# Three blocks of each down projection in Strassen's way, half of the weight sums made by adding transfers

## The chip, the core and the metric

The kernel runs on one core of one Trainium2 chip. The metric is device time in microseconds of one execution, as the median of several runs. The core has five engines that matter here: TensorE (PE; its weight loads are PEld), VectorE (DVE), ScalarE (ACT), GpSimd (POOL) and SyncE (SP), which issues most of the transfers. Sixteen DMA engines carry out the transfers of all queues. SBUF is the working memory; PSUM holds eight banks of 128 x 512 float32 into which PE accumulates.

## The reference

The program is a two-layer decoder trunk on 256 tokens of width 1024, in float32. Each layer has a half-step SwiGLU FFN, a mixing stage (two kinds of attention side by side), a second half-step FFN, and a gated embedding:

```
h = h + 0.5 * (silu(norm(h) @ Wg) * (norm(h) @ Wu)) @ Wd     # FFN 1, width 2816
h = h + concat(stick_breaking(u), latent_attention(u)) @ Wo   # u = norm(h)
h = h + 0.5 * FFN2(norm(h))
h = h + sigmoid(norm(h) @ Wpg) * (p[i] @ Wp)
```

The change concerns the product with Wd (2816 x 1024), the down projection, which occurs four times: FFN "a" and FFN "b" of two layers.

## The kernel before

Every float32 product is made of three: each operand x is split into a high part xh (x rounded to the type that PE reads) and a rest xl = x - xh, and `mm3` (L176 to L178) issues xh*yh, xh*yl and xl*yh into one PSUM bank. The weights arrive as float32 and are split on the core. A *unit* is 2048 columns of 128 rows, in two pieces of 1024 (512 KB). `Unit.load` issues the transfer of a piece on SP's queue into a tile of the pool `raw` (four buffers, L126), copies it to `wh` on ScalarE (L130) and subtracts into `wl` on VectorE (L131); `wh` and `wl` have six buffers each. One piece is one *chunk* of the down projection: 128 rows of Wd by all 1024 columns.

`ffn` first makes the gates, in six blocks of 512 of the 2816 columns (the last has 256). Per block it runs `g` and `u` matmuls for two token halves (t = 0, 1; 128 tokens each). `gated` multiplies silu(g) by u, and `Gates.add` turns the result over: four transposes on PE into a bank `ft` (L373), a copy into `fh` (L376), a subtract into `fl` (L377). So block i of the gates lies in SBUF as 4 chunks of 128 rows by 256 tokens.

Then comes the down projection with four PSUM banks `d[t][n]` (token half t, column half n). Per chunk, `down_mm` issues 2 x 3 matmuls for each token half, 12 in all. After the first two chunks `flush` runs what is still due of the gates; `lagging` runs the other 20 chunks, the second token half three chunks behind the first, so that the residual step of the first half (L313, `h` plus half of `d`, then norm and transposes) overlaps matmuls of the second.

The order of instructions is not simply that of the program. A planner at build time places instructions on each engine by program order among those that it holds ready, grants buffers, and adds the waits. `soon`, `tick` and `flush` delay some steps by an estimated PE time; `after` adds a pure order edge. Once built, each engine runs its list in order; SP's transfers wait in SP's list for their buffer.

`ple_inputs` (L757 to L763) loads and splits the embedding input p of the layer; it stands in the program between the mixing stage and FFN b. The mixing stage keeps its latent tiles under tags of their own: `cq`, `xq`, `ckv`, `xkv`, `qr`.

Of the kernel before, what the change touches and what calls it, by code (L numbers as in the profile page):

```python
# [9 lines left out]
F32 = mybir.dt.float32  # L10
F32R = mybir.dt.float32r
# [6 lines left out]
P = 128  # L18
# [12 lines left out]

F_TAGS = ("sbq", "sbk", "v", "vm", "n0h", "n0l", "n1h", "n1l", "f4h", "f4l", "f5h", "f5l")
# [11 lines left out]
def trunk(ctx: ExitStack, tc: tile.TileContext, xT, xr, pT, w, gains, fgain, consts, out):  # L44
# [3 lines left out]
    raw_p = pool("raw", 4)  # L48
# [58 lines left out]
    class Unit:  # L107
# [36 lines left out]
        def at(self, k, c0, c1):  # L144
            q, o = k // self.per, k % self.per * self.cols
            i = o * self.sub // PIECE
            if (q, i) not in self.here:
                self.here.add((q, i))
                self.load(q, i)
            return tuple(t[:, o + c0 : o + c1] for t in self.parts[q])  # L150

# [4 lines left out]
    def soon(us, f):  # L156
        due.append((pe[0] + us, len(due), f))
# [23 lines left out]
    def both(x, *ix):  # L181
        return tuple(t[ix] for t in x)
# [161 lines left out]
    class Gates:  # L344


        def __init__(self, tag):
            self.tag, self.f = tag, {}
# [14 lines left out]

        def add(self, i, t, pr, more):

            f = self.block(i)
            n = 4 if i < NBLK - 1 else 2

            def go():
                a = bank(f"ft_{self.tag}_{i}{t}")[:, : n * P]  # L370
                behind = newest_mm[0]
                for j in range(n):
                    after(nc.tensor.transpose(a[:, j * P : (j + 1) * P], pr[:, j * P : (j + 1) * P], ident), behind)  # L373
                a = a.rearrange("p (a b) -> p a b", a=n)
                fh, fl = both(f, slice(None), slice(None), slice(t * P, (t + 1) * P))
                nc.scalar.activation(fh, a, AF.Copy)  # L376
                nc.vector.tensor_tensor(fl, a, fh.bitcast(F32), ALU.subtract)  # L377

            soon(1.3 + 0.9 * t + more, go)

    def ffn(x, n, tag, gcol, between=None, feed=None):
# [13 lines left out]
        for i in range(NBLK):  # L395
# [42 lines left out]
            for r in rests:  # L438
                r()
        if between is not None:  # L440
            between()
        d = four(f"d_{tag}")
        us = [Unit(2) for _ in range(DFF // 256)]
        chunks = [(us[k // 2], k % 2, k) for k in range(DFF // P)]
        for c in range(2):
            u, j, k = chunks[c]
            for t in range(2):
                down_mm(d, u, j, gates(k), gates.at(k), t, c == 0, False)
        flush()
        return lagging(chunks[2:], d, gates, 0.5, tag, gcol, 3, False)  # L450

    def mix(x, n, L, g0):
# [93 lines left out]
        cq = at_p.tile([P, 2, T], F32, tag="cq", name=f"cq{L}")  # L546
        nc.vector.tensor_tensor(cq, la, bc(rstd, 2), ALU.mult)
        xq = tuple(at_p.tile([P, 2, T], F32R, tag=f"xq{q}", name=f"xq{q}{L}") for q in "hl")
# [10 lines left out]
        ckv = at_p.tile([P, 1, T], F32, tag="ckv", name=f"ckv{L}")  # L559
        nc.vector.tensor_tensor(ckv[:, 0], la[:, 0], rstd, ALU.mult)  # L560
        xkv = tuple(at_p.tile([P, 1, T], F32R, tag=f"xkv{q}", name=f"xkv{q}{L}") for q in "hl")
# [81 lines left out]
        qr = at_p.tile([P, 2, T], F32, tag="qr", name=f"qr{L}")  # L643
# [113 lines left out]
    def ple_inputs(L):  # L757
        pr = at_p.tile([P, 2, T], F32, tag="cq", name=f"p{L}")
        nc.sync.dma_start(pr, pT[L])
        xp = tuple(at_p.tile([P, 2, T], F32R, tag=f"xq{q}", name=f"xp{q}{L}") for q in "hl")  # L760
        nc.scalar.activation(xp[0], pr, AF.Copy)
        nc.vector.tensor_tensor(xp[1], pr, xp[0].bitcast(F32), ALU.subtract)
        return xp  # L763
# [74 lines left out]
    for L in range(DEPTH):  # L838
# [3 lines left out]
        xp = ple_inputs(L)  # L842
        x, n = ffn(x, n, f"b{L}", g0 + G_PLE)
# [10 lines left out]
def _weights(i):  # L854
# [9 lines left out]
    for L in range(DEPTH):  # L864
# [5 lines left out]
        def ffn(n):  # L870
# [7 lines left out]
            units.extend(cols(wd[k : k + 256], ar(DM)) for k in range(0, DFF, 256))  # L878
# [81 lines left out]
```

## Time and profile before

| | |
|---|---|
| median of 3 runs | 1039.98 us (1039.97 to 1040.15) |
| the profiled execution | 1040.93 us |
| its span in the profile | 1039.1 us |
| TensorE busy | 1022.7 us, 98% |
| VectorE busy | 616.4 us, 59% |
| ScalarE busy | 571.2 us, 55% |
| GpSimd busy | 8.2 us, 1% |
| read from memory | 185.45 MB, 179 GB/s over the span |

"Busy" is the time in which an engine had at least one instruction in work. Matmuls are pipelined: a row gives each 0.39 us, while the next one starts before it ends. In rows of a timeline the first number is the start in the span, the second the length, and the bracket says how long the engine had been idle and what ended that. In rows of groups, "x176 | 69.2, 393 | 0.0" is the count, the busy sum, the mean in ns and the idle time before.

### The profile page before, as it was taken

Reading aid. Unit: us, or ns where it says so; the run is one execution under the profiler, and the core shown is the slowest. Engines: PE = TensorE matmul, PEld = TensorE weight load, DVE = VectorE, ACT = ScalarE, POOL = GpSimd, SP = SyncE. Lnnn points to the kernel's source line nnn. Section 1 sums busy time; section 2 is a strip of 40 time slices with the busy share of each in tenths; the row PEclk is TensorE's granted clock in tenths of the full one; section 3 lists DMA queues with packets and bytes.
Section 4 is the critical chain, followed back from the end, with each engine's and each line's share of the span. In section 5 each row is a group of like instructions: output and inputs, shape, how many; then the busy total and the mean of one; then the engine's idle time right before and its main releaser. Section 6 shows DMA issues by size and latency. Waiting matters only on the chain.

```text
span 1039.1 us, 13656 instructions
## 1 busy us (share of the span) xinstructions
PE 1022.7 (98%) x5178; PEld 863.3 (83%) x5178; DVE 616.4 (59%) x855; ACT 571.2 (55%) x869; POOL 8.2 (1%) x13
## 2 busy tenths in 40 slices
PE   9999999999999999999999999999999999999996
PEld 7688888899888888888888888888997888888885
DVE  5565544766776555546875555448677755554475
ACT  5854444758565544435764455347766744444464
POOL 0000000000100000000000000000000000000000
PEclk9999999999999999999999999999999999999998
DMA  7775545565146555555465555456633465554551
GB/s 235 282 245 185 184 158 195 192 216 178 64 147 205 190 183 184 181 164 201 165 219 186 182 183 182 164 199 215 209 107 111 144 219 184 184 182 162 189 197 40
DMA packets 53490, 187.39 MB, mean 180 GB/s; under 512 B 6064, under 2 KB 6192, under 8 KB 53424
## 3 DMA queue, kind: packets, MB, share of 16 engines
q1 hardware_dynamic: 52992, 185.95, 53.7%
q8 instruction: 40, 0.66, 0.3%
q10 hardware_dynamic: 432, 0.57, 0.2%
q14 instruction: 26, 0.21, 0.1%
HBM read 185.45 MB, written 1.05 MB: 179 GB/s over the span
## 4 chain that ended last, share of the span: by engine, by line
PE 91%; ACT 3%; DMA 2%; DVE 2%; issue 1%; SPq 0%; ACTq 0%
PE g_b L178 4%; PE g_b L176 4%; PE g_b L177 4%; PE d_b L177 4%; PE d_b L178 4%; PE d_b L176 4%; PE d_a L176 4%; PE d_a L177 4%; PE d_a L178 4%; PE g_a L178 4%; PE g_a L176 4%; PE g_a L177 4%; PE u_b L176 3%; PE u_b L177 3%; PE u_b L178 3%; PE u_a L177 3%
## 5 line engine op out<-in xcount | busy, mean ns | idle before, releaser
L131 DVE TENSOR_TENSOR wl<-raw,wh 128x1024 fp32r<-128x1024 f32 (+1 forms) x354 | 424.1, 1202 | 351.6 <-ACT wh L130 350.7
L130 ACT ACTIVATE wh<-raw 128x1024 fp32r<-128x1024 f32 (+1 forms) x354 | 366.6, 1041 | 366.3 <-PE d_a L178 64.4
L176 PE MATMUL d_a<-wh,fh_a 128*128 128x512 f32 x176 | 69.2, 393 | 0.0
L176 PE MATMUL d_b<-wh,fh_b 128*128 128x512 f32 x176 | 69.2, 393 | 0.0
L178 PE MATMUL d_a<-wh,fl_a 128*128 128x512 f32 x176 | 68.6, 390 | 0.0
L178 PE MATMUL d_b<-wh,fl_b 128*128 128x512 f32 x176 | 68.6, 390 | 0.0
L177 PE MATMUL d_a<-wl,fh_a 128*128 128x512 f32 x176 | 68.5, 389 | 0.0
L177 PE MATMUL d_b<-wl,fh_b 128*128 128x512 f32 x176 | 68.5, 389 | 0.0
L178 PEld LDWEIGHTS d_a<-wh,fl_a 128*128 128x128 f32 x176 | 33.0, 188 | 7.0
L178 PEld LDWEIGHTS d_b<-wh,fl_b 128*128 128x128 f32 x176 | 33.0, 188 | 6.9
L177 PEld LDWEIGHTS d_a<-wl,fh_a 128*128 128x128 f32 x176 | 33.1, 188 | 6.7
L176 PEld LDWEIGHTS d_b<-wh,fh_b 128*128 128x128 f32 x176 | 33.0, 188 | 6.6
L177 PEld LDWEIGHTS d_b<-wl,fh_b 128*128 128x128 f32 x176 | 33.1, 188 | 6.6
L176 PE MATMUL g_b<-wh,x_mix1h 128*128 128x512 f32 x96 | 38.4, 400 | 0.0
L176 PE MATMUL g_b<-wh,x_mix0h 128*128 128x512 f32 x96 | 38.4, 400 | 0.0
L176 PEld LDWEIGHTS d_a<-wh,fh_a 128*128 128x128 f32 x176 | 33.1, 188 | 6.5
L176 PE MATMUL g_a<-wh,xe0h 128*128 128x512 f32 x96 | 38.4, 400 | 0.0
L176 PE MATMUL g_a<-wh,x0h 128*128 128x512 f32 x96 | 38.1, 398 | 0.3 <-ACT x0h L221 0.3
L177 PE MATMUL g_a<-wl,x0h 128*128 128x512 f32 x96 | 37.5, 393 | 0.3 <-DVE wl L131 0.2
L178 PE MATMUL g_a<-wh,xe0l 128*128 128x512 f32 x96 | 37.5, 391 | 0.0
L178 PE MATMUL g_b<-wh,x_mix0l 128*128 128x512 f32 x96 | 37.5, 390 | 0.0
L178 PE MATMUL g_b<-wh,x_mix1l 128*128 128x512 f32 x96 | 37.5, 390 | 0.0
(383 smaller groups left out, 2282.8 us busy)
## 6 DMA issues: line engine op xcount, KB each, us to landing
raw<-in_w SPq DMA_DIRECT2D x338, 512.0 KB, 3.6
raw<-in_w SPq DMA_DIRECT2D x16, 256.0 KB, 4.0
xin<-in_xT SPq DMA_DIRECT2D x4, 256.0 KB, 3.5
h<-in_xr SPq DMA_DIRECT2D x2, 512.0 KB, 7.6
p<-in_pT SPq DMA_DIRECT2D x2, 256.0 KB, 4.5
fg<-in_fgain SPq DMA_DIRECT2D x1, 512.0 KB, 3.2
out_h<-hg SPq DMA_DIRECT2D x2, 256.0 KB, 2.3
out_h<-hg ACTq DMA_DIRECT2D x2, 256.0 KB, 2.7
```

Source lines behind the costliest of these rows:

```text
L130: nc.scalar.activation(wh[:, a], r[:, a], AF.Copy),
L131: nc.vector.tensor_tensor(wl[:, a], r[:, a], wh[:, a].bitcast(F32), ALU.subtract),
L176: nc.tensor.matmul(o, ah, bh, start=start, stop=False, **kw)
L177: nc.tensor.matmul(o, ah, bl, start=False, stop=False, **kw)
L178: newest_mm[0] = nc.tensor.matmul(o, al, bh, start=False, stop=stop, **kw)
```

## The change

In blocks 1, 2 and 3 of each FFN, four chunks (512 rows of Wd) are treated as one product of 256 x 512 activations by 512 x 1024 weights, cut in half in each direction. Winograd's form of Strassen's scheme makes it of 7 products of a quarter (each 128 tokens x 256 rows x 512 columns, six matmuls) instead of 8. Products 2, 3 and 4 go straight into three of the `d` banks; products 1, 5, 6 and 7 get a bank each, summed over the three blocks, and are combined once after the third.

- *Activations.* `Gates.sums` forms four sums of quarters after the transposes of token half 1 (one copy and four VectorE instructions of 128 x 512, then two copies and two subtracts as splits). Those of blocks 1 and 2 lie in a pair of the x buffers, those of block 3 in new tiles `s0h`, `s0l`. For token half 1, only the second two chunks of these blocks are still split.
- *Weights.* `Seven` loads the four quarters b11, b12, b21, b22 (512 KB each, stored as such), and makes 7 operands: b11, b22, b21 as loaded, b12 + b22, b11 + b12, that plus b22, and that plus b21; the signs are taken into the activations. The first two sums are made by transfers issued on POOL that add a quarter from memory to the tile (`accum_op`), the last two by VectorE. Each operand is copied and subtracted as before.
- *Order.* Two plain chunks, block 1, two plain chunks, block 2, the two chunks of the short last block, block 3, the combination into `h`, then the four chunks of block 4 in `lagging`. The weights in memory follow this order.
- *Room.* `raw` has six buffers instead of four; the latent tiles and p move under the tags `s0h`, `s0l`, `s1h`, `s1l`; the scratch for transfers issued by POOL is set to 2048; `ple_inputs` now runs behind the combination of FFN b.

```diff
-    raw_p = pool("raw", 4)
+    raw_p = pool("raw", 6)
...
+    class Seven:
...
+        def load(self, i):
+            self.raw[i] = raw_p.tile([P, PIECE], F32, tag="raw", name=f"raw7_{self.u}_{i}")
+            newest_load[0] = nc.sync.dma_start(self.raw[i], self.home(i))
...
+        def fetch(self, i, j):
+            nc.gpsimd.dma_start(self.raw[i], self.home(j), accum_op=ALU.add)
+        def add(self, i, j):
+            nc.vector.tensor_tensor(self.raw[i], self.raw[i], self.raw[j], ALU.add)
+        def parts(self, i):
...
+            newest_wh[0] = nc.scalar.activation(wh, r, AF.Copy)
+            nc.vector.tensor_tensor(wl, r, wh.bitcast(F32), ALU.subtract)
+            return wh, wl
+        def operands(self):
+            b11, b12, b21, b22 = range(4)
+            self.load(b12)
+            self.fetch(b12, b22)
+            self.load(b11)
+            yield 1, self.parts(b11)
+            self.fetch(b11, b12)
+            self.load(b22)
+            yield 3, self.parts(b22)
+            self.load(b21)
+            yield 2, self.parts(b21)
+            yield 7, self.parts(b12)
+            yield 5, self.parts(b11)
+            self.add(b11, b22)
+            yield 6, self.parts(b11)
+            self.add(b11, b21)
+            yield 4, self.parts(b11)
...
+    def seven_mm(banks, x_of, ops, first, last):
+        for p, (wh, wl) in ops:
+            for j in range(2):
+                c = slice(j * 512, (j + 1) * 512)
+                mm3(banks[p], x_of(p, j), (wh[:, c], wl[:, c]), first(p) and j == 0, last(p) and j == 1, skip_group_check=True)
...
+        head, tail = block(0), block(NBLK - 1)
+        plain(head[:2], True)
+        flush()
+        p = {2: d[0][0], 3: d[0][1], 4: d[1][0]}
+        p.update((i, bank(f"p{i}_{tag}")) for i in (1, 5, 6, 7))
+        own = (1, 5, 6, 7)
+        for i in SEVEN:
+            seven_mm(p, gates.seven(i), Seven().operands(), lambda q: q in own and i == SEVEN[0], lambda q: q in own and i == SEVEN[-1])
+            if i != SEVEN[-1]:
+                plain(head[2:] if i == SEVEN[0] else tail)
...
+        u, v, a, b = (flat(f"w{k}", f"{m}7_{tag}") for k, m in enumerate("uvab"))
+        nc.scalar.copy(u, p[1])
+        nc.vector.tensor_tensor(u, u, p[6], ALU.add)
+        to_h(0, 0, p[1])
+        nc.vector.tensor_tensor(v, u, p[7], ALU.add)
+        to_h(1, 0, v)
+        nc.vector.tensor_tensor(a, p[5], u, ALU.subtract)
+        to_h(0, 1, a)
+        nc.vector.tensor_tensor(b, p[5], v, ALU.subtract)
+        to_h(1, 1, b)
         if between is not None:
             between()
...
+        rest = [c for i in range(1, NBLK - 1) if i not in SEVEN for c in block(i)]
+        return lagging(rest, d, gates, 0.5, tag, gcol, 3, False)
...
-    nc = bacc.Bacc("TRN2", target_bir_lowering=False, num_devices=1)
+    nc = bacc.Bacc("TRN2", target_bir_lowering=False, num_devices=1, dynamic_dma_scratch_size=2048)
```

More of the change, by code (lines that the diff above doesn't have):

```diff
@@ L362, in at, with sums, seven, of @@
             return k % 4
+        def sums(self, i):
+            a, b = self.turned[i, 0], self.turned[i, 1]
+            lo, hi = slice(0, 2), slice(2, 4)
+            e = SEVEN.index(i)
+            if e == 0:
+                self.spare = tuple(x_p.tile([P, KC, T], F32R, tag=f"x{q}", name=f"sx{q}_{self.tag}") for q in "hl")
+            if e < 2:
+                out = both(self.spare, slice(None), slice(4 * e, 4 * e + 4))
+            else:
+                out = tuple(f_p.tile([P, 4, T], F32R, tag=f"s0{q}", name=f"s{q}_{self.tag}_{i}") for q in "hl")
+            two = [wt(f"w{2 + k}", f"sum{k}_{self.tag}_{i}") for k in range(2)]
+            s1, s2, s3, s4 = (two[k // 2][:, k % 2].rearrange("p (a b) -> p a b", a=2) for k in range(4))
+            nc.scalar.copy(s3, b[:, lo])
+            nc.vector.tensor_tensor(s1, s3, b[:, hi], ALU.subtract)
+            nc.vector.tensor_tensor(s2, s1, a[:, lo], ALU.subtract)
+            nc.vector.tensor_tensor(s3, a[:, lo], s3, ALU.subtract)
+            nc.vector.tensor_tensor(s4, s2, a[:, hi], ALU.add)
+            for k in range(2):
+                sh, sl = both(out, slice(None), slice(2 * k, 2 * k + 2))
+                nc.scalar.activation(sh, two[k], AF.Copy)
+                nc.vector.tensor_tensor(sl, two[k], sh.bitcast(F32), ALU.subtract)
+            self.s[i] = out
+        def seven(self, i):
+            f, s = self.f[i], self.s[i]
+            t0, t1 = slice(0, P), slice(P, T)
+            def of(p, j):
+                if p in (1, 2, 4):
+                    return both(f, slice(None), j + 2 * (p != 1), t1 if p == 4 else t0)
+                return both(s, slice(None), {5: 0, 6: 1, 7: 2, 3: 3}[p], slice(j * P, (j + 1) * P))
+            return of
         def add(self, i, t, pr, more):
@@ L642, in mix @@
         nc.vector.tensor_tensor(r2, qs[3], bc(rc[:, 1], 2), ALU.mult)
-        qr = at_p.tile([P, 2, T], F32, tag="qr", name=f"qr{L}")
+        qr = at_p.tile([P, 4, T], F32, tag="s1l", name=f"qr{L}")[:, 0:2]
         nc.gpsimd.tensor_tensor(qr, r1, r2, ALU.add)
@@ L877, in ffn, with down @@
             wide(np.concatenate([wg[:, m], wu[:, m]], axis=1), ar(512))
-            units.extend(cols(wd[k : k + 256], ar(DM)) for k in range(0, DFF, 256))
+            def down(b):
+                units.extend(cols(wd[k : k + 256], ar(DM)) for k in range(512 * b, min(512 * b + 512, DFF), 256))
+            down(0)
+            down(NBLK - 1)
+            for b in SEVEN:
+                for k in (512 * b, 512 * b + 256):
+                    units.append(np.concatenate([cols(wd[k : k + 256], ar(c, c + 512)) for c in (0, 512)], axis=1))
+            for b in range(1, NBLK - 1):
+                if b not in SEVEN:
+                    down(b)
         ffn("ffn1")
```

57 lines of the change are left out of this document (36 added, 21 removed).

## The prediction

> **What bounds the kernel now.** I read the page's busy times and its chain of waits first, then stretches of the down projections, then single instructions there.
>
> ```profile
> span 1039.1 us, 13656 instructions
> ...
> PE 1022.7 (98%) x5178; PEld 863.3 (83%) x5178; DVE 616.4 (59%) x855; ACT 571.2 (55%) x869; POOL 8.2 (1%) x13
> ...
> PE 91%; ACT 3%; DMA 2%; DVE 2%; issue 1%; SPq 0%; ACTq 0%
> ```
>
> TensorE is the bound: 98% busy, 91% of the chain. A matmul taken out shortens the kernel, as long as nothing else becomes late. The next view gives stretches (length, then busy time of PE, PEld, DVE, ACT, POOL, the granted clock, the DMA share, GB/s): the middle of the first down projection, a gate stretch with more work around it, and the fullest stretch of transfers.
>
> ```profile
> 140.00:185.00 45.00, 45.00 (x201) 37.24 (x200) 18.81 (x17) 15.91 (x15) 0.00 (x0) 1.00 0.56 184
> 45.00:66.00 21.00, 21.00 (x102) 17.41 (x101) 17.84 (x21) 15.56 (x19) 0.00 (x0) 1.00 0.80 263
> 25.00:40.00 15.00, 14.67 (x64) 11.27 (x62) 7.24 (x14) 9.28 (x17) 0.00 (x0) 1.00 0.96 367
> ```
>
> In the down projection PE never stops, at full clock, while VectorE works 42% and the DMA engines 56% of the time. The second row shows that VectorE at 85% (17.84 of 21.00) still cost PE nothing.
>
> A matmul's row says 0.39 us, but matmuls overlap; what one costs is the distance of their starts:
>
> ```profile
> 185.62 1.06 ACT L130 ACTIVATE wh<-raw 128x1024 fp32r<-128x1024 f32 x1 [1.66 <-PE d_a L178]
> 185.64 0.39 PE L177 MATMUL d_a<-wl,fh_a 128*128 128x512 f32 x1
> ...
> 187.00 0.39 PE L177 MATMUL d_a<-wl,fh_a 128*128 128x512 f32 x1
> ...
> 188.34 1.06 ACT L130 ACTIVATE wh<-raw 128x1024 fp32r<-128x1024 f32 x1 [1.66 <-PE d_a L178]
> ```
>
> The two PE rows are six matmuls apart (each third one has L177, and one of that line lies between): 1.36 us, so 0.227 us each. ScalarE takes a new chunk every 2.72 us, the 12 matmuls of a chunk, and waits each time for PE to give a pair of weight buffers back:
>
> ```profile
> ACT wh L130 <- PE d_a L178: 64.4, 34, 5.7
> ```
>
> So weights are converted six pairs ahead of PE. This lead is what the change spends.
>
> **The matmuls.** A block of four plain chunks is 48 matmuls, 10.88 us. In Strassen's way it is 7 products of 6: 42, or 9.52 us. Three blocks in each of four FFNs: 12 x 1.36 = **16.3 us less**. Against the profiled execution (1040.93 us, 1.83 beyond its span) that is 1024.6; against the median of the runs, 1039.98, it is 1023.7. I carry the differences to the median.
>
> **VectorE and ScalarE in such a block.** The prices:
>
> ```profile
> L131 DVE TENSOR_TENSOR wl<-raw,wh 128x1024 fp32r<-128x1024 f32 x338 | 413.4, 1227 | 339.8 <-ACT wh L130 339.1
> L130 ACT ACTIVATE wh<-raw 128x1024 fp32r<-128x1024 f32 x338 | 356.5, 1060 | 356.9 <-PE d_a L178 64.4 <-PE d_b L178 64.4 <-PE u_b L178 44.9
> ...
> L390 DVE SCALAR_TENSOR_TENSOR pr_b<-u_b,hr_mix,s_b 128x512 f32<-128x512 f32 x20 | 14.0, 743 | 0.0
> ...
> L377 DVE TENSOR_TENSOR fl_a<-ft_a,fh_a 128x512 fp32r<-128x512 f32 x20 | 13.7, 687 | 1.7 <-ACT fh_a L376 0.8
> ...
> L376 ACT ACTIVATE fh_a<-ft_a 128x512 fp32r<-128x512 f32 x20 | 11.8, 590 | 5.9 <-PE ft_a L373 5.9
> ```
>
> Seven operands instead of four are copied and subtracted, and two sums are added by VectorE (a 128x1024 add, priced as the subtract): 9 x 1.23 = 11.1 us of VectorE and 7 x 1.06 = 7.4 of ScalarE, beside 9.52 of PE. VectorE is over PE inside the block; with the two plain chunks that follow (2.46 against 5.44) it is 13.5 against 14.96. Throughput holds over a period; order and latency decide.
>
> **The transfers.** Landing times of 512 KB loads, in the stretches 25 to 40, 45 to 66 and 140 to 185 us:
>
> ```profile
> raw<-in_w SPq DMA_DIRECT2D x6, 512.0 KB, 6.7
> ...
> DMA to landing us min/median/max: 4.2/6.7/8.0
> ...
> raw<-in_w SPq DMA_DIRECT2D x11, 512.0 KB, 4.6
> ...
> raw<-in_w SPq DMA_DIRECT2D x15, 512.0 KB, 4.3
> ```
>
> At share 0.96 the engines moved 367 GB/s, so a full rate of 382: 1.37 us for 512 KB. Landing is 4.3 us at share 0.56, 4.6 at 0.80, 6.7 at 0.96. A period after the change has six loads and two adding transfers. The trace has no adding transfer and none issued by POOL. If adding costs as a load, the share is 8 x 1.37 / 14.96 = 0.73; if it also reads what it adds to, 10 x 1.37 / 14.96 = 0.92. I take the row at 0.80, 4.6 us, for a load, and X = 4.6 + 1.37 (the second reading) + 0.33 (an issue, as SP's below) = **6.3 us** for an adding transfer from its release to its landing. Its bounds: below, the fastest load of this stretch, 4.2; above, 6.7 + 1.37 + 0.33 = 8.4.
>
> [...]
>
> **The chain that becomes late.** In one block the tile of b11 goes: load, copy and subtract (product 1), adding transfer, copy and subtract (5), add, copy and subtract (6), add, copy and subtract (4). Its next use needs a buffer: of six raw tiles the block holds four and the plain chunks two, so the next block's b11 waits for the one that the first add gives back. Written out with the prices above, zero being PE's start on the first plain chunk:
>
> ```
>                           block 1   block 2   block 3
> b11 landed (+4.6)          early     10.84     27.70
> product 1 subtracted       early     13.28     30.14
> sum landed (+6.3)          early     19.58     36.44
> pair 5 ready / wanted       5.0/10.9  21.9/25.8  38.7/40.8
> first add done              6.24     23.10     39.96
> pair 6 ready / wanted       8.5/12.2  25.4/27.2  42.3/42.2
> pair 4 ready / wanted      12.1/13.6  28.9/28.6  45.8/43.5
> ```
>
> ("Wanted" is PE undelayed: the blocks start at 5.44, 20.40 and 35.36, products 1.36 us apart. In block 1 the copy of pair 5 starts when the first chunk's pair is free, 2.72.) The lead is eaten in blocks 1 and 2; block 3's last product comes 2.3 us late. What is queued behind a late sum: on ScalarE the copies, on VectorE the subtracts of the same pairs, then those of the next plain chunks. PE has other work meanwhile, the last block's chunks for the first token half, which write other banks than product 4 (d[1][0]) but need subtracts of the same VectorE: I take half as covered, 1.1 us lost per FFN.
>
> **After the third block** one copy and seven VectorE instructions (about 0.69 each by L377) put the products into h: 4.8 us, beside four plain chunks (10.88 of PE, 4.9 of VectorE). They fit, but stand ahead of those chunks in the program: from 0 to 4.8 us; I take 0.4, since the sum of 9.7 is under 10.88.
>
> So 1.5 us of each 4.08 are lost: 4 x 2.6 = 10.3 us gained.
>
> **Costed at nothing.** The sums of activations add six VectorE instructions of 0.69 and three ScalarE ones of 0.59 per block, less half of one split: VectorE goes from 8 x 1.23 + 2 x 0.74 + 2 x 0.69 = 12.7 to 16.5 us in the 21.8 of a gate block's 96 matmuls, 76%, under the 85% that cost nothing above; uncovered, 3.8 us per block. All eight banks are in use from block 1: the last transposes must be read out before product 5 or 6; uncovered, under 2 us per FFN. Half of the x buffers, and the tags shared with the latent tiles, are last read by products long done. The inputs p move behind the products (per layer 0.33 us of SP, 0.63 of ScalarE, 0.68 of VectorE, needed only a stage later); their rows, and one of the output projection wo:
>
> ```profile
> L759 SPq DMA_DIRECT2D p<-in_pT x2: 327/327/327, 247.5 to 758.2; - x2
> L761 ACT ACTIVATE xph<-p x2: 627/627/627, 267.4 to 778.1; 128x512 fp32r<-128x512 f32 x2
> L762 DVE TENSOR_TENSOR xpl<-p,xph x2: 674/675/676, 271.8 to 782.6; 128x512 fp32r<-128x512 f32 x2
> ...
> L176 PE MATMUL wo<-wh,y0h x32: 389/389/499, 276.4 to 303.6; 128*128 128x512 f32 x32
> ```
>
> In the program they stand behind all of wo, whose first matmul is at 276.4, yet the load ran at 247.5 and the split at 267.4 and 271.8: the planner takes what is ready. So I expect SP's loads for the last block ahead of the new p load, which must wait until block 3's sums of activations are read.
>
> **Rivals.**
> 1. *Everything hides*: X is 4.6 or less. Gain 16.3: 1023.7. For: VectorE's 13.5 of 14.96. Against: landing at share 0.80 is 4.6 already without adding.
> 2. *The gain is eaten*: each us of X comes twice by block 3 (blocks 2 and 3), so the loss is 1.5 + 2 (X - 6.3); it reaches 4.08 at X = 7.6: 1040. The p load held in program order ends there too: the last block's loads behind it would start with product 6's end, 43.5, and land and convert by 43.5 + 0.3 + 4.6 + 2.3 = 50.7 against 44.9 wanted, 5.8 us in two FFNs, 11.7 together: 1041.
> 3. *Slower, the sums land too late*: past X = 7.6 the wait for the adding transfer, on ScalarE's copy of pair 5, takes the place of PE. At X = 8.4 the loss is 5.7 per FFN, 1.6 more than the gain: 1046.5. For: 6.7 us at share 0.96 and a share of up to 0.92 here; the planner's order is fixed ahead, so ready subtracts stand behind the late one. Against: the lead of six pairs.
>    [...]
> 4. *Much slower, the adding itself*: an adding transfer that keeps the engines five times as long needs 16 x 1.37 = 21.9 us in each period of 14.96: three times 6.9 less 4.08, four times: +67, 1107. Nothing in the trace speaks for it or against it.
>
> **Numbers.** My forecast of 10.3 us, **1029.7**, has 0.44, with 1025.5 to 1037.5 as its own range (X from 5.3 to 7.2, or the h sums half exposed). Rival 1 has 0.20, rival 2 0.08, rival 3 0.20, rival 4 0.08. A measurement of this kernel can tell about 0.2%, 2.1 us, from no change. Faster: 0.44 + 0.20 = 0.64; same 0.08; slower 0.28. The range runs from full hiding, 1023.5, to rival 3's 1046.5; outside lie rival 4 and part of rival 3, under 0.2.
>
> **What would show it.** The matmuls fall by 12 x 6 = 72 from 5178. Right: PE without idle in block 1, idle of about 1.5 us at the end of block 3, ended by a subtract; adding transfers landing in 5.3 to 7.2 us. Rival 1: none of that idle. Rivals 3 and 4: ScalarE's copies ended by DMA in every block 2 and 3, and a DMA share over 0.9. Wrong altogether: idle in the gate stretches (the activation sums), or SP's loads behind p in the second and fourth FFN.

## The result: slower by 5.3%, and the profile after

The changed kernel takes **1095.09 us** (median of 4 runs, 1094.97 to 1097.6) against 1040.07 us for the kernel before in the same session: a ratio of 1.0527, with a 95% interval of 1.0514 to 1.0539. Forecast were 1029.7 us, and 1023.5 to 1046.5 as the range. The profiled execution took 1095.11 us, 54.2 more than the profiled one of before. Its page, cut to the lines that answer to those shown of before:

```profile
span 1093.3 us, 13847 instructions
...
PE 1040.9 (95%) x5106; PEld 861.7 (79%) x5106; DVE 731.8 (67%) x1019; ACT 617.9 (57%) x945; POOL 28.3 (3%) x37
...
q1 hardware_dynamic: 52992, 185.95, 50.7%
q0 software_dynamic: 3456, 12.58, 6.7%
...
PE 73%; DVE 10%; ACT 7%; DMA 6%; issue 3%; SPq 0%; ACTq 0%; DVEq 0%
...
raw<-in_w SPq DMA_DIRECT2D x338, 512.0 KB, 4.1
raw<-in_w POOLq DMA_DIRECT2D x24, 512.0 KB, 7.0
```

The matmuls fell by 72, as they should. But PE's share of the chain fell from 91% to 73%, and VectorE, ScalarE and DMA share 23%: PE is no longer the bound all the way. Where this happens the four down projections show, each from its first matmul to the first of the next stage. First the kernel before (its sum over the four), then the kernel after; columns as in the prediction: length, busy PE, PEld, DVE, ACT, POOL, granted clock, DMA share, GB/s.

```profile
sum 245.40, PE 245.40 PEld 203.03 DVE 117.86 ACT 111.35 POOL 0.00; mean PE 61.35 PEld 50.76 DVE 29.46 ACT 27.84 POOL 0.00
```

```profile
133.00:205.50 72.50, 64.38 (x260) 48.69 (x260) 51.25 (x56) 36.17 (x47) 3.46 (x4) 0.93 0.65 184
440.80:516.30 75.50, 66.75 (x260) 51.43 (x259) 52.45 (x60) 36.98 (x47) 3.45 (x4) 0.89 0.66 188
670.80:742.40 71.60, 63.45 (x260) 48.35 (x259) 51.17 (x56) 36.02 (x46) 3.46 (x4) 0.95 0.64 185
979.30:1055.40 76.10, 66.91 (x260) 50.66 (x259) 52.19 (x60) 37.00 (x47) 3.47 (x4) 0.89 0.65 187
sum 295.70, PE 261.49 PEld 199.13 DVE 207.06 ACT 146.18 POOL 13.85; mean PE 65.37 PEld 49.78 DVE 51.77 ACT 36.54 POOL 3.46
```

295.7 against 245.4: the down projections lost 50.3 us where 16.3 were to be gained. PE stood idle for 34.2 us, and was busy for 32.4 us more than the 229.1 that the matmuls need (245.4 - 16.3), at a clock of 0.89 to 0.95. VectorE is busy for 70% of the stretch and the DMA engines for 65%, so neither is full on average. While the adding transfers of blocks 2 and 3 run, though, the DMA engines are all but full. Here are the two of the first FFN, from issue to landing; over the other six the share is 0.91 to 0.99 too:

```profile
150.05:157.52 7.47, 7.47 (x34) 6.18 (x34) 3.59 (x3) 2.09 (x3) 0.86 (x1) 1.00 0.99 243
171.30:179.25 7.95, 7.95 (x37) 6.58 (x36) 3.45 (x3) 2.01 (x2) 0.86 (x1) 1.00 0.96 240
```

The rest of the loss is in the mixing stage, from its first matmul to that of the next gates, before and then after, two layers:

```profile
sum 216.70, PE 213.08 PEld 193.38 DVE 154.65 ACT 144.21 POOL 7.75; mean PE 106.54 PEld 96.69 DVE 77.33 ACT 72.11 POOL 3.88
```

```profile
sum 221.60, PE 215.61 PEld 194.72 DVE 152.97 ACT 142.91 POOL 6.93; mean PE 107.81 PEld 97.36 DVE 76.49 ACT 71.46 POOL 3.47
```

That is 4.9 us; 50.3 + 4.9 less 1.0 in other stages makes the 54.2.

What sets the pace of a down projection stands in the chain of waits of the first FFN (start, length, what):

```profile
148.62 1.14 DVE wl L181
150.05 7.47 DMA raw<-in_w
...
157.63 1.07 ACT wh L180
158.72 1.24 DVE wl L181
159.98 1.24 DVE raw L175
...
165.28 1.06 ACT wh L180
...
167.51 0.79 DVE wl L133
168.65 1.22 DVE wl L133
169.87 1.15 DVE wl L181
171.30 7.95 DMA raw<-in_w
```

Read from the top: product 1's subtract of block 2 lets the adding transfer into b11 start (150.05); its sum is copied and subtracted (product 5), added to (L175), copied and subtracted (6), added to, copied and subtracted (4, from 165.28), then **two plain chunks are subtracted (L133)**, and only then comes product 1's subtract of block 3 and the next adding transfer, 21.25 us after the first. In the other three FFNs it is 21.35, 20.65 and 21.41 us. PE's work for such a period is 14.96 us. VectorE's own list shows that the two plain subtracts stand ahead of the next product 1 at the first boundary too:

```profile
145.12 1.23 DVE L181 TENSOR_TENSOR wl<-raw,wh 128x1024 fp32r<-128x1024 f32 x1 [1.21 <-ACT wh L180]
146.26 2.36 DVE L133 TENSOR_TENSOR wl<-raw,wh 128x1024 fp32r<-128x1024 f32 x2
148.53 1.22 DVE L181 TENSOR_TENSOR wl<-raw,wh 128x1024 fp32r<-128x1024 f32 x1
```

ScalarE's list has the copies of the two plain chunks ahead of product 1's copy in the same way (145.00, then 146.89).

### The profile page after: what moved, and what is told of

It reads as the page before. It is cut to its first block, busy times and chain, and to the rows that moved or that the text cites. A ratio compares the mean times of both kernels' runs of the same rounds, so it can differ in the third digit from the quotient of the medians.

```text
span 1093.3 us, 13847 instructions
## 1 busy us (share of the span) xinstructions
PE 1040.9 (95%) x5106; PEld 861.7 (79%) x5106; DVE 731.8 (67%) x1019; ACT 617.9 (57%) x945; POOL 28.3 (3%) x37
## 3 DMA queue, kind: packets, MB, share of 16 engines
q1 hardware_dynamic: 52992, 185.95, 50.7%
## 4 chain that ended last, share of the span: by engine, by line
PE 73%; DVE 10%; ACT 7%; DMA 6%; issue 3%; SPq 0%; ACTq 0%; DVEq 0%
DMA raw<-in_w 5%; PE g_b L229 4%; PE g_b L227 4%; PE g_b L228 4%; DVE wl L181 4%; PE u_b L229 3%; PE u_b L228 3%; PE u_b L227 3%; PE g_a L229 3%; PE g_a L227 3%; PE g_a L228 3%; ACT wh L180 3%; PE u_a L228 3%; PE u_a L229 3%; PE u_a L227 3%
## 5 line engine op out<-in xcount | busy, mean ns | idle before, releaser
L133 DVE TENSOR_TENSOR wl<-raw,wh 128x1024 fp32r<-128x1024 f32 (+1 forms) x306 | 362.9, 1197 | 185.0 <-ACT wh L132 181.7
L132 ACT ACTIVATE wh<-raw 128x1024 fp32r<-128x1024 f32 (+1 forms) x306 | 312.6, 1035 | 190.6 <-PE u_b L229 50.2
L180 ACT ACTIVATE wh<-raw 128x1024 fp32r<-128x1024 f32 x84 | 87.5, 1057 | 134.6 <-DVE raw L175 60.8
L181 DVE TENSOR_TENSOR wl<-raw,wh 128x1024 fp32r<-128x1024 f32 x84 | 101.6, 1224 | 87.4 <-ACT wh L180 87.4
L228 PE MATMUL d_a<-wl,fh_a 128*128 128x512 f32 x104 | 42.1, 405 | 3.2 <-DVE wl L133 1.7
L229 PE MATMUL d_a<-wh,fl_a 128*128 128x512 f32 x104 | 41.6, 400 | 0.0
L228 PE MATMUL g_b<-wl,x_mix0h 128*128 128x512 f32 x96 | 37.4, 390 | 0.0
L228 PE MATMUL g_b<-wl,x_mix1h 128*128 128x512 f32 x96 | 37.4, 390 | 0.0
L228 PE MATMUL g_a<-wl,xe0h 128*128 128x512 f32 x96 | 37.4, 390 | 0.0
L229 PE MATMUL g_a<-wh,x0l 128*128 128x512 f32 x96 | 37.3, 390 | 0.0
```

What stands on the lines that cost most here:

```text
L132: nc.scalar.activation(wh[:, a], r[:, a], AF.Copy),
L133: nc.vector.tensor_tensor(wl[:, a], r[:, a], wh[:, a].bitcast(F32), ALU.subtract),
L180: newest_wh[0] = nc.scalar.activation(wh, r, AF.Copy)
L181: nc.vector.tensor_tensor(wl, r, wh.bitcast(F32), ALU.subtract)
L228: nc.tensor.matmul(o, ah, bl, start=False, stop=False, **kw)
L229: newest_mm[0] = nc.tensor.matmul(o, al, bh, start=False, stop=stop, **kw)
```

## The experiments

All times are medians, of two runs for pool_plain and dve_add and of four or more for the others; the ratio is to the kernel before, timed beside it.

| run | what differs | us | ratio, 95% |
|---|---|---|---|
| after | | 1095.09 | 1.0527 [1.0514, 1.0539] |
| no_add | after, the two first sums left out | 1038.83 | 0.9989 [0.9968, 1.0010] |
| pool_plain | after, POOL's transfers copy | 1080.41 | 1.0382 [1.0330, 1.0434] |
| dve_add | after, all sums on VectorE | 1072.98 | 1.0311 [1.0281, 1.0341] |
| pool_sums | after, two sums on GpSimd | 1081.34 | 1.0394 [1.0378, 1.0409] |
| filled | after, PE given filling work | 1103.90 | 1.0607 [1.0592, 1.0623] |
| late_h | after, sums into h later | 1089.51 | 1.0468 [1.0444, 1.0493] |
| early1 | after, product 1's pair earlier | 1064.04 | 1.0224 [1.0208, 1.0240] |
| early1_late | both | 1067.24 | 1.0237 [1.0202, 1.0272] |
| three_pool | three blocks, three remedies | 1075.00 | 1.0335 [1.0318, 1.0352] |
| one_block | Strassen in block 2 alone | 1043.41 | 1.0027 [1.0016, 1.0038] |
| two_between | blocks 1, 3; six chunks between | 1047.08 | 1.0065 [1.0050, 1.0080] |
| two_inner | blocks 1, 3; chunks inside | **1029.82** | 0.9899 [0.9883, 0.9916] |
| two_inner_dve | the same, all sums on VectorE | **1028.30** | 0.9883 [0.9869, 0.9898] |
| raw6 | before, six raw buffers | 1040.87 | 1.0001 [0.9992, 1.0010] |
| shared_tiles | before, latent tiles shared | 1047.98 | 1.0071 [1.0056, 1.0086] |

### Are the sums the cause, and how they are made?

**no_add.** The two first sums of each block are not made; b12 and b11 stay as loaded.

```diff
         def fetch(self, i, j):
-            nc.gpsimd.dma_start(self.raw[i], self.home(j), accum_op=ALU.add)
+            pass
```

> Two of the four sums of weights are left out: no adding transfer, all else as changed. Theory A (the chain load, product 1, adding transfer of some 7.9 us from release to landing, product 5, is longer than PE's period; the drop of the clock follows from PE's idle time): the period of the chain falls from 21.3 us to 21.3 - 7.9 = 13.4, under PE's 14.96, so blocks 2 and 3 are no longer late; what stays is the sums into h in front of the last chunks, up to 4.8 us per FFN: 1024 to 1042, granted clock near 0.997. Theory B (VectorE's added work and the h sums are what is late, the transfers only run beside them): 1075 or more.

1038.8 us: 56 us less than the kernel after. Everything else that the change brought (activation sums, VectorE's two adds, banks, sums into h, moved tiles) stays, and the down projections shrink to 60.1, 58.5, 58.1 and 59.3 us, near the 57.3 of the matmuls alone (229.1 / 4). That the kernel is not faster still is due to its mixing stages, 224.3 us together and 7.6 more than before. The loss in the down projections belongs to the first two sums, or to what waits for them.

**pool_plain.** The same transfers on the same queue, as copies.

```diff
-            nc.gpsimd.dma_start(self.raw[i], self.home(j), accum_op=ALU.add)
+            nc.gpsimd.dma_start(self.raw[i], self.home(j))
```

> The two transfers per block stay on GpSimd's queue, but copy instead of adding (so these two sums are left out). Theory A with the wait as such: a plain transfer keeps the engines 1.56 us instead of 3.05, so each lands 1.5 us sooner, which comes twice per FFN and more with the clock: 1075 to 1088. If adding itself is what is slow: near the run without transfers, 1024 to 1042. If issuing from GpSimd is what is slow: 1090 to 1096. Theory B: 1090 to 1096.

```profile
raw<-in_w POOLq DMA_DIRECT2D x24, 512.0 KB, 4.7
```

A copy lands in 4.7 us instead of 7.0. The kernel takes 1080.4: that the transfer adds explains about 15 us of the 55. It is still 42 us over no_add, with a plain transfer at this place in the chain. The next run takes that away too.

**dve_add.** b12 is loaded by SP, and all four sums are VectorE's; no transfer stands inside the chain.

```diff
         def operands(self):
-            self.load(b12)
-            self.fetch(b12, b22)
             self.load(b11)
             yield 1, self.parts(b11)
-            self.fetch(b11, b12)
+            self.load(b12)
+            self.add(b11, b12)
             self.load(b22)
             yield 3, self.parts(b22)
+            self.add(b12, b22)
             self.load(b21)
             yield 2, self.parts(b21)
```

> All four sums on VectorE, no adding transfers. Theory A: the chain has an add of 1.23 us in place of 7.9, but VectorE has 11 instructions of 1.23 per block, 13.5 us, and 16.0 in a period of 14.96: 1 us late per period and the h sums exposed: 1035 to 1060. Theory B: two more VectorE instructions per block make it worse than the change: 1100 to 1125.

1073.0 missed both. Without any transfer to wait for, 33 us are lost all the same. So "the sum lands too late", my rival 3, is no full account. Groups of waits of this run:

```profile
ACT wh L180 <- DVE raw L175: 76.1, 27, 3.9
```

ScalarE waits for each sum before it can copy, 27 times, 2.8 us on average, while VectorE then waits for the copy. In the first FFN the subtracts of product 1 in blocks 2 and 3 start at 149.32 and 168.50: a period of 19.2 us without a transfer in it, with the two plain subtracts still ahead of them.

**pool_sums.** The two first sums by GpSimd.

```diff
+        def padd(self, i, j):
+            nc.gpsimd.tensor_tensor(self.raw[i], self.raw[i], self.raw[j], ALU.add)
...
+            self.load(b12)
+            self.padd(b11, b12)
...
             yield 3, self.parts(b22)
+            self.padd(b12, b22)
             self.load(b21)
```

> The kernel after with the two adding transfers replaced by plain loads of b12 and two adds on GpSimd (128x1024, estimated 2 x 1.28 us from the 128x512 add of the trace), all three blocks. The chain from product 1's subtract to product 4's pair is then 2.5 + 2.3 + 1.2 + 2.3 + 1.2 + 2.3 = 11.9 us instead of 17.9, VectorE does as much as in the kernel after. Theory A (the chain's length decides): a period of 15 to 17 us, 1035 to 1058 with the mixing stage's 5 us. Theory B (what decides is VectorE with its waits for ScalarE's copies, as it was with all sums on VectorE): 1060 to 1085.

```profile
L178 POOL TENSOR_TENSOR raw<-raw,raw x24: 2398/3256/3267, 126.9 to 1013.6; 128x1024 f32<-128x1024 f32 x24
```

An add took 3.26 us (median), not the 2.5 that I estimated, and both were in the chain one behind the other. 1081.3: the range of theory B, but for a reason that it did not name. So the three ways of making the sums give 1073 to 1095 us, and in the first FFN periods of 21.25 (adding transfers), 19.2 (VectorE) and 21.27 us (GpSimd, from 149.77 to 171.04), all of them over PE's 14.96. At the block boundaries they have the order of the work in common, which the next runs change.

### Does the chain have to be this long?

**early1.** In the program, the loads of b12 and b11, the adding transfer into b12 and product 1's pair of the next block stand ahead of the two plain chunks, PE's order unchanged.

```diff
+        sevens = [Seven().operands() for _ in SEVEN]
+        ahead = {SEVEN[0]: []}
-        for i in SEVEN:
-            seven_mm(p, gates.seven(i), Seven().operands(), lambda q: ...
+        for e, i in enumerate(SEVEN):
+            seven_mm(p, gates.seven(i), itertools.chain(ahead[i], sevens[e]), lambda q: ...
             if i != SEVEN[-1]:
+                ahead[SEVEN[e + 1]] = [next(sevens[e + 1])]
                 plain(head[2:] if i == SEVEN[0] else tail)
```

> The kernel after with the loads of b12 and b11, the adding transfer into b12 and the first pair (product 1's) of blocks 2 and 3 put ahead of the two plain chunks before the block, in the program; TensorE's order stays. If the two plain subtracts (2.4 us) that stood ahead of product 1's subtract are part of the chain, it shortens to 18.9 us: 2 x 2.4 x 4 = 19 us less, 1073 to 1080, and more if the earlier transfer into b12 helps. If the transfer alone sets the chain: 1090 to 1097.

1064.0: **31 us less, by the order of the work alone**, more than the 19 expected. VectorE at the boundary, the two adding transfers in the chain of waits, and the down projections' sum:

```profile
144.64 2.36 DVE L181 TENSOR_TENSOR wl<-raw,wh 128x1024 fp32r<-128x1024 f32 x2 [1.21 <-ACT wh L180]
146.91 2.35 DVE L133 TENSOR_TENSOR wl<-raw,wh 128x1024 fp32r<-128x1024 f32 x2
```

```profile
147.29 7.90 DMA raw<-in_w
...
166.69 7.68 DMA raw<-in_w
```

```profile
sum 262.00, PE 245.02 PEld 192.53 DVE 196.66 ACT 142.25 POOL 10.37; mean PE 61.25 PEld 48.13 DVE 49.17 ACT 35.56 POOL 2.59
```

The two L181 in one piece are block 1's last and block 2's first pair, and the plain ones come behind. The adding transfer is released at 147.29 here, 14.7 us after the down projection began (132.6); in the kernel after at 150.05, 17.05 after its beginning (133.0). The next one follows after 19.40 us instead of 21.25, and the plain subtracts are gone from the chain. The loads and the transfer into b12, which the edit moves too, are not in the chain of this FFN, before or after the edit. The sum of the down projections falls by 33.7 us to 262.0, still 16.6 over the kernel before. Of the 33.7, 17.2 are idle time of PE and 16.5 are matmuls that run faster, since the mean clock of the execution rises from 0.973 to 0.988: a part of the gain comes by way of the clock. The mixing stage is no better than after.

**late_h.** The combination into h moved behind the first plain chunks of block 4.

```diff
-    def lagging(chunks, d, x, scale, tag, gcol, lag, first=True):
+    def lagging(chunks, d, x, scale, tag, gcol, lag, first=True, hook=None):
...
         for i in range(N + lag):
+            if hook is not None and i == 2:
+                hook()
...
```

> The kernel after with the eight operations that put the products into h moved behind the first plain chunks that follow the third block, nothing else. If they lie on the path in full (4.7 us of idle TensorE seen at the end of the third block): 4 x 4.7 = 19 us less, 1074 to 1080. If the plain chunks would be late anyway, because no subtract is ready ahead: 1085 to 1097.

1089.5: 5.6 us less, 1.4 per FFN, not 4.7. Inside the down projections more was gained: in the profiled execution they are 284.7 us together, 11.0 less than after, while the mixing stages are 226.7, 5.1 more. That these operations stand in front of the first plain subtract is plain in VectorE's list of the kernel after. In the first FFN PE was then still at product 4 and lost 0.78 us to that subtract; in the second it lost 3.5, and in all four 7.2:

```profile
188.41 0.69 DVE L570 TENSOR_TENSOR u_a<-u_a,p_a 128x512 f32<-128x512 f32 x1 [1.34 <-PE p_a L229]
...
193.15 1.22 DVE L133 TENSOR_TENSOR wl<-raw,wh 128x1024 fp32r<-128x1024 f32 x1
```

```profile
194.42 0.50 PE L228 MATMUL d_a<-wl,fh_a 128*128 128x512 f32 x1 [0.78 <-DVE wl L133]
```

**early1_late.** Both edits together.

> As the run early1, with the sums into h moved as in the run late_h. If the two gains are of different waits they add up: 5 to 8 us less than early1, 1065 to 1075. If the plain chunks after the block are late anyway: the same as early1 within 3 us.

1067.2, within 3 us of early1: no further gain. With product 1 early, moving the sums into h gains nothing that can be told here.

**three_pool.** Three blocks with GpSimd's adds, the late combination, the latent tiles and p as before, and five raw buffers instead of six, for room.

> Three blocks with GpSimd's adds as in the run pool_sums, the sums into h moved as in the run late_h, the latent tiles and the inputs p as in the kernel before, and five raw buffers instead of six for room. If the three losses add up: 5 us of the mixing stage and some us of the h sums less than pool_sums, 1024 to 1045. If five raw buffers or the adds hold it back: over 1050.

1075.0: 6 us less than pool_sums, so the losses do not simply add up. In the profiled execution the down projections take 268.1 us, 14.5 less than in pool_sums, but the mixing stages 222.4, as long as there (222.7) although the latent tiles are as before. Which of the five buffers and the adds holds it back was not separated.

### Is it the clock?

**filled.** Eight matmuls with weights of zero behind products 7, 5 and 6 of blocks 2 and 3.

```diff
+            if idle is not None and p in (7, 5, 6):
+                for _ in range(8):
+                    nc.tensor.matmul(banks[p], zr, idle, start=False, stop=False, skip_group_check=True)
...
```

> The kernel after with eight matmuls of a zero weight tile behind each of the products 7, 5 and 6 in blocks 2 and 3, 1.8 us of TensorE each, 10.9 us per FFN: they add zeros, so what is computed stays, and TensorE has something to do while a sum is awaited. Theory C (half of the loss is the clock, which drops after TensorE has stood idle): the granted clock stays at 0.99 or more, a down projection takes 57.2 (the work) plus 10.9 (the filling) plus the h sums' 4.7 at most, 68 to 73 us instead of 71.5 to 76, and the kernel 1070 to 1088. Theory D (the clock does not matter, because the chain of sums sets the period of a block and TensorE only waits for it): within 3 us of the kernel after, 1092 to 1098, with the clock up. Theory E (the clock drop does not come from idling): the clock stays at 0.97 and the time goes to 1095 to 1140.

```profile
132.80:207.40 74.60, 70.43 (x307) 57.28 (x306) 52.56 (x61) 36.52 (x48) 3.45 (x4) 0.98 0.65 191
...
984.60:1062.10 77.50, 70.98 (x308) 57.31 (x307) 52.63 (x60) 37.33 (x49) 3.47 (x4) 0.96 0.62 187
sum 303.80, PE 282.58 PEld 229.23 DVE 209.57 ACT 147.83 POOL 13.82; mean PE 70.64 PEld 57.31 DVE 52.39 ACT 36.96 POOL 3.45
```

The clock rises from 0.89 to 0.95 to 0.96 to 0.98, PE does 192 matmuls more (43.6 us at 0.227), and the down projections take 8.1 us more. Of the 43.6 us, 13.0 come out of idle time (34.2 to 21.2) and 22.5 out of the other matmuls, whose busy time is 239.0 us at the higher clock (282.6 - 43.6) instead of 261.5. The period of a block is what it was: in the first FFN the adding transfers go out at 149.81 and 171.14, 21.33 us apart, in the others 21.47, 20.55 and 21.81. So the clock does not set the period, as theory D has it; E falls, since the mean clock rose to 0.986. Theory C would have the down projections at 68 to 73 us each; they are at 74.5 to 77.5, but its number is not a clean test. PE waits here for the residual step ahead of its transposes, 18.1 us in four waits that the kernel after does not have: in the first FFN five plain subtracts stand ahead of the sums into h in VectorE's list, where the kernel after has them behind. These waits are more than the 8.8 us by which the kernel is slower than after. What the slow clock costs behind block 3, outside of the period, this run does not tell.

### Can the chain be covered?

**one_block.** Strassen in block 2 alone, behind two plain chunks, with 16 plain chunks after it.

```diff
-SEVEN = (1, 2, 3)
+SEVEN = (2,)
...
```

> Strassen's way for block 2 alone in each FFN, with its two adding transfers, sixteen plain chunks behind it. Theory A: as in block 1 of the prediction's table its pairs are ready before they are wanted, and the h sums lie beside 16 chunks: 4 x 1.36 = 5.4 us gained, 1034.6 to 1037. Theory B: the h sums and the order still cost 3 us or more per FFN: 1045 or more.

1043.4, outside both ranges. The down projections did take what was expected, 60.1 us each, 1.3 less than before; but the mixing stage took 112.0 us in both layers instead of 108.3. One block costs nothing in its own stage, and the change has a second cost elsewhere.

**two_between.** Blocks 1 and 3, six plain chunks between them, latent tiles and p as before.

```diff
-SEVEN = (1, 2, 3)
+SEVEN = (1, 3)
+GAP = 6
...
-                plain(head[2:] if i == SEVEN[0] else tail)
+                plain(queue[pos : pos + GAP])
+                pos += GAP
...
```

> Two Strassen blocks (1 and 3) with six plain chunks between them and none inside; adding transfers, the sums into h straight behind the last block as in the kernel after; latent tiles and inputs p as in the kernel before. Theory A (a block's chain of 21.25 us has to fit into the period of the blocks, here 9.5 + 6 x 2.72 = 25.8 us, wherever the plain chunks lie): hidden, 1029 to 1035, the upper end if the sums into h are exposed by 1 us each. Theory B (the sums must be covered inside the block, where product 4 is wanted 8.2 us after product 1 and came 17.9 after it): idle of 2 to 8 us in each block, 1040 to 1070.

1047.1: theory A, my favourite, missed, though 25.8 us of PE work are in each period. The chain of waits at the second block of the first FFN:

```profile
148.17 4.81 DMA raw<-in_w
...
153.09 1.07 ACT wh L182
154.18 1.24 DVE wl L183
155.70 9.22 DMA raw<-in_w
...
173.95 0.04 DVE wl L183
```

b11's load starts when a plain chunk six tiles earlier gives its raw buffer back (148.17), and product 1's pair is ready at 155.4. PE wants product 1 at 163.9 (132.6 + 8 chunks x 2.72 + 9.52) and product 4 8.2 us later, at 172.1; product 4's pair is ready at about 175.2, 19.8 us after product 1's. So 3.1 us are late; this down projection is 62.0 us long, 3.5 more than that of two_inner below, which has the same matmuls. Its only idle times of PE are the 1.30 and 0.76 us in front of product 4, so the sums into h, which two_inner moves as well, are not the difference in it. Plain chunks ahead of a block don't help beyond the lead that the buffers allow: 8.5 us here.

**two_inner.** The same two blocks, with one plain chunk behind each of the products 7, 5 and 6 *inside* the block, two between, and the combination into h late.

```diff
+            def chunk(q):
+                if q in (7, 5, 6):
+                    plain(queue[pos[0] : pos[0] + 1])
+                    pos[0] += 1
...
+GAP = 2
...
+                plain(queue[pos[0] : pos[0] + GAP])
+                pos[0] += GAP
...
```

> Two Strassen blocks (1 and 3) in place of three, a plain chunk laid behind each of the products 7, 5 and 6, inside the block, two plain chunks between the blocks, the sums into h moved behind the first plain chunks that follow, the latent tiles and the inputs p as in the kernel before; adding transfers as in the kernel after. If the loss was the chain of sums being longer than the work laid beside it (period of 21.25 us seen, work here 9.5 + 5 x 2.7 = 23.1 us per block), the chain is covered: 8 x 1.36 = 10.9 us gained, 1029 to 1033. If adding transfers cost something else (VectorE slowed, transfers slowed for all), over 1040.

```profile
132.80:191.30 58.50, 58.50 (x265) 48.42 (x264) 45.70 (x54) 34.15 (x43) 1.73 (x2) 1.00 0.71 225
...
sum 234.30, PE 234.30 PEld 193.79 DVE 181.56 ACT 135.34 POOL 6.93; mean PE 58.58 PEld 48.45 DVE 45.39 ACT 33.84 POOL 1.73
```

**1029.8 us, faster than both kernels.** PE never stops, the clock stays at 1.00, and the down projections are 11.1 us shorter than before; 8 x 1.36 = 10.9 were expected. From product 1's start to product 4's PE now has 8.2 + 3 x 2.72 = 16.3 us of work, beside a chain of 18 to 20, and the lead covers the difference. ScalarE still waits for the transfers, and it costs nothing:

```profile
ACT wh L182 <- DMA raw<-in_w: 22.6, 10, 4.6
```

**two_inner_dve.** The same kernel with the sums as in dve_add.

> The kernel of the run two_inner with all four sums of a block made by VectorE and b12 loaded plainly, no adding transfer. If a sum that is covered is free whoever makes it (VectorE then has 16 x 1.23 = 19.7 us of work in a period of 23.1): 1028 to 1032, as two_inner. If VectorE's turns with ScalarE are longer than the cover, as in the run dve_add: 1035 to 1050.

1028.3, the same as two_inner within the intervals. Where the chain is covered, the adding transfers bring nothing over VectorE's adds, in spite of 4 x 1.23 instead of 2 x 1.23 us per block.

### The mixing stage

**raw6** (six raw buffers in the kernel before) and **shared_tiles** (its latent tiles under the shared tags, as in the change), both with the scratch of the change:

```diff
-    raw_p = pool("raw", 4)
+    raw_p = pool("raw", 6)
...
```

```diff
-        cq = at_p.tile([P, 2, T], F32, tag="cq", name=f"cq{L}")
+        lat = at_p.tile([P, 4, T], F32, tag="s0h", name=f"lat{L}")
+        cq, ckv = lat[:, 0:2], lat[:, 2:3]
...
-        pr = at_p.tile([P, 2, T], F32, tag="cq", name=f"p{L}")
+        pr = at_p.tile([P, 4, T], F32, tag="s0h", name=f"p{L}")[:, 0:2]
...
```

> The kernel before with six raw buffers instead of four and the smaller scratch for descriptors, no Strassen block. If the mixing stage lost its time to loads that run further ahead (six raw tiles let the transfers bunch), its stretch from v to the first gate block grows by 1.5 to 4 us per layer: 1043 to 1048. If it lost it to the shared tiles or to what the changed FFN leaves behind, nothing moves: 1038.5 to 1041.

> The kernel before with the latent tiles of the mixing stage (cq, ckv, xq, xkv, qr, p, xp) in the shared tiles of four blocks, as in the kernel after, four raw buffers, no Strassen block; the smaller scratch for descriptors makes room. If sharing delays the mixing stage: 1043 to 1048. If the prediction was right that the sharing costs nothing: 1038.5 to 1041.

1040.9 and 1048.0: the buffers cost nothing, the sharing alone 7.4 us. The sum of its two mixing stages, and what PE waits for ahead of the output projection in the first of them, before and with the shared tiles:

```profile
sum 223.60, PE 216.42 PEld 195.74 DVE 154.86 ACT 144.19 POOL 7.78; mean PE 108.21 PEld 97.87 DVE 77.43 ACT 72.09 POOL 3.89
```

```profile
PE wo L176 <- ACT y0h L221: 1.4, 1, 1.4
```

```profile
PE wo L176 <- ACT y0h L221: 3.3, 1, 3.3
```

The two stages are 6.9 us longer than before; the profiled execution as a whole is 5.2 longer (1046.17), so the loss is all here. Half of it, 3.6 us, is idle time of PE (length less busy time), nearly all in this wait and its like in the second layer (3.3 instead of 1.5). The other 3.3 are matmuls that take longer, at a granted clock of 0.98 in both stages instead of 1.00. In the kernel after the stage lost 4.9, with waits of 2.8 us. Which of the shared tiles delays `y0h` was not tried. Nor is sharing all: three_pool does not share, its two waits are back at 1.4 and 1.5 us, and its mixing stages are still 5.7 us longer than before. This stayed open.

## Why the prediction was wrong, point by point

**Right.** 72 matmuls fewer, and 1.36 us per block to be had: two_inner gets 11.1 us from 8 blocks. The activation sums and the banks cost nothing that shows: in the kernel after the gate stretch of the second FFN is 125.3 us long, as before, and no_add, which keeps all of them, has its down projections at 236.0 together, 6.9 over their matmuls. The new load of p went out at 495.03, behind five loads for the last block, and held nothing. An adding transfer landed 7.0 us after its issue in the median (5.2 to 8.4); with the 0.28 us from release to issue, which the prediction's X includes, that is 7.3, inside the bounds of 4.2 to 8.4 and just over the 5.3 to 7.2 named for the forecast. A plain copy on this queue took 4.7 in the median (pool_plain). Rival 4 was not at work: an adding transfer kept the engines 3.05 us, about twice the 1.56 of a load, not five times (last section).

**The step that failed: the table of the chain, in its order on VectorE.** Its rows for blocks 2 and 3 let product 1's subtract follow right behind product 4's of the block before (its 12.1 and 28.9, unrounded: 12.05 + 1.23 = 13.28; 28.91 + 1.23 = 30.14), and its text puts the subtracts of the plain chunks behind. The prediction had read the planner as taking what is ready (from the rows of p). But VectorE's list as it ran has the program's order at this place: block 1's product 4 first (145.12), then two plain chunks (146.26), then product 1 (148.53). The times from PE's first plain chunk, predicted and seen in the first FFN:

| | predicted | seen |
|---|---|---|
| block 1, pair 4 ready | 12.1 | 13.3 |
| block 2, product 1 subtracted | 13.28 | 16.8 |
| block 2, sum landed | 19.58 | 24.5 |
| block 2, pair 4 ready (wanted 28.6) | 28.9 | 34.6 |
| block 3, product 1 subtracted | 30.14 | 38.0 |
| block 3, pair 4 ready (wanted 43.5) | 45.8 | 57.2 |

Block 1 was right to 1.2 us. Product 1 of block 2 is then 3.5 us late, by these 1.2 and by the two plain subtracts. The period, 16.86 in the table, is 21.25. Of these 4.4 us, 2.8 are the order: between the first add and the end of product 1's subtract the table counts two pairs, one add and that subtract, 2.29 + 1.23 + 2.29 + 1.23 = 7.04 us; by the chain it is 9.8 (161.2 to 171.0), with the two plain subtracts in it. The adding transfer is 1.5 (7.8 from the subtract that releases it to its landing, where I had 6.3). Each is small, but with a period above PE's 14.96 the lateness grows from block to block, and once the lead is eaten nothing hides it. early1 shows the size of the order: 31 of the 55 us. X alone would not have led there: with 7.8 in the prediction's own formula, 1.5 + 2 (X - 6.3), the loss is 4.5 us per FFN and the kernel 1041.7.

**A second step failed with it: "I take half as covered".** The prediction had block 3's last product 2.3 us late and charged 1.1. In the first FFN of the kernel after it was 13.7 us late (57.2 against 43.5), and the down projection took 15.2 more than its 57.3 us of matmuls; in early1 it was 8.5 late and 8.4 were lost. Nothing was covered.

**Rival 3 came nearest, with a part of the mechanism and the wrong size.** ScalarE's copies did wait for transfers (45.4 us in 20 waits), for the adding ones 25.8 us in six of the eight blocks 2 and 3, and while these ran the DMA share was 0.91 to 0.99: both of its signs nearly as foretold. But dve_add loses 33 us with no transfer in the chain. The rival varied X alone; the order was held right in all of them, and that left 1095 out of the range.

**Sums into h**: 0.4 us per FFN costed. PE lost 1.8 to the first plain subtract behind them (7.2 in four), and moving them gained 1.4 (late_h), or 2.7 in the down projections alone; nothing in early1_late. A small miss. After the result I read 4.7 off VectorE's list, and that was too much: PE was behind at that time.

**"The tags shared with the latent tiles" costed at nothing**: 7.4 us on their own (shared_tiles); the mixing stage of the kernel after lost 4.9, which three_pool shows not to be the tags alone. I asked only whether the last readers are done, not what the new order of grants does to the stage that takes the tiles.

**Not considered: the clock.** After stretches with waits PE ran at a granted clock of 0.50 for 55 us in all (six stretches of 3.4 to 17.1 us). filled shows that it does not set the period of a block. Behind the last block the slow matmuls do lie on the chain (in the fourth FFN they follow each other by 0.43 us instead of 0.23 from 1042 to 1047), and what this made of the 55 us was not separated.

**What stays open.** early1 is 24 us over before: 16.6 in the down projections, which are still 32.9 over their matmuls, and 7.8 in the mixing stage. The first part is the same chain at a period of 19.40: the adding transfer at 147.29 takes 8.2 us from the end of product 1's subtract, 1.9 over the prediction's X, and product 4 of block 3 is 8.5 us late. That two_inner hides all of it fits this: the chain's length against the work beside it. The part in the mixing stage is not explained. No form of three blocks that hides the chain was run: 10 plain chunks per FFN are too few to lay three in each block and keep the last four.

## What to carry to other kernels

Before you price a chain of dependent steps, write down each engine's list in its order and let every step wait for its predecessor *there*, not only for its data; a period longer than the work beside it (21.25 us against 14.96 here) is lost again in every round. Cover for such a chain has to lie between its first and its last use: work laid ahead of it helps only as far as the buffers let the chain start early (two_between: 8.5 us of lead, 1047.1 us; two_inner: 1029.8). Read a share where the chain waits and not over the stage: the DMA engines' 0.65 was 0.91 to 0.99 there. And a saving that fits with room in two places (1030 us) beats one that just closes in three (1095).

## What the runs showed of the hardware

An adding transfer kept the DMA engines about twice as long as a load: q0's 6.7% of 1093.3 us over 24 transfers are 3.05 us of all 16 engines each; q1's 50.7% over 185.95 MB are 1.56 us per 512 KB. As copies (pool_plain) the same transfers of POOL take 1.5 us of the engines each (3.3% of 1076.4 us over 24) and land in 4.7 us instead of 7.0, where SP's loads of the kernel after took 4.1 (medians).

At the end of block 3 in the first FFN of the kernel after, the granted clock fell to 0.50 though PE had work in each of these stretches of 3.4 us:

```profile
180.80:184.20 3.40, 1.61 (x6) 0.86 (x5) 2.60 (x3) 0.79 (x2) 0.00 (x0) 0.98 0.02 10
184.20:187.60 3.40, 2.53 (x5) 1.74 (x6) 2.45 (x2) 0.79 (x2) 0.00 (x0) 0.50 0.44 154
187.60:191.00 3.40, 3.25 (x7) 1.46 (x7) 2.60 (x4) 3.40 (x5) 0.00 (x0) 0.50 0.47 154
191.00:194.40 3.40, 2.64 (x7) 1.55 (x5) 3.40 (x6) 2.85 (x4) 0.00 (x0) 0.52 0.46 154
194.40:197.80 3.40, 3.38 (x15) 2.78 (x16) 3.40 (x4) 0.16 (x1) 0.00 (x0) 1.00 0.55 170
```

After a stretch with 1.61 of 3.40 us busy the granted clock was 0.50 to 0.52 for three stretches, though PE was busy for 2.5 to 3.3 us in each of them, and it came back only at 194.4. No single idle time of PE between 180.8 and 184.6 was longer than 1.5 us. The fourth FFN shows the same: after a stretch with 1.62 of 3.40 us busy (1027.2 to 1030.6) the clock is 0.50 for five stretches, and matmuls follow each other there (1042 to 1047) by 0.43 us instead of 0.23. Apart from its last 5 us, the whole trace has the clock at half for six stretches, of 10.2, 10.2, 6.8, 6.8, 3.4 and 17.1 us, and in the 3.4 us ahead of each PE was busy for 0.89 to 1.79 us. Which part of the waits brings the clock down was not shown.
